# Multiplying the first group's last 256 columns between two pieces of the second group, in a log-softmax backward kernel

## Chip, cores, metric

One core of a Trainium2 chip. The metric is the device time of the whole kernel in microseconds (us), as the median of several executions.

## The reference

```python
# y, dy: (8, 1024, 8192) float32
softmax_x = np.exp(y)
sum_dy = np.sum(dy, axis=-1, keepdims=True)
return (dy - softmax_x * sum_dy).astype(np.float32)
```

Each row needs the sum of its own dy before any of it can be multiplied. 537 MB are read and 268 MB written.

## The kernel before

The 8192 rows are 32 groups of 256 rows, two rows (r = 0, 1) on each of 128 partitions, so a group's dy, y and output are 8.39 MB each. Groups go in pairs: the even one in tile x0, the odd one in x1; one y tile serves both. The product is formed in place in x. All transfers are issued on one queue (SP).

```python
PIECES = [(0, 2048), (2048, 5120), (5120, D)]          # D = 8192, W = 2 * D
def sums(x): ...      # -sum(dy): row 0 on VectorE (reduce), row 1 on ScalarE (two copies that accumulate)
def compute(x, s_t, r):
    for b, e in PIECES:
        cs = slice(r * D + b, r * D + e)
        nc.scalar.activation(y_t[:, cs], y_t[:, cs], EXP)
        nc.vector.scalar_tensor_tensor(out=x[:, cs], in0=y_t[:, cs], scalar=s_t[:, r : r + 1],
                                       in1=x[:, cs], op0=ALU.mult, op1=ALU.add)
for g in range(0, G, 2):
    load_dy(g, x_ts[0])
    load_y(g, 0, W)
    s_t = sums(x_ts[0])
    for r in range(R):
        compute(x_ts[0], s_t, r)
    load_dy(g + 1, x_ts[1])
    s_t = sums(x_ts[1])
    for r in range(R):
        load_y(g + 1, r * D, (r + 1) * D)              # y_t is free once the even group has used it
        compute(x_ts[1], s_t, r)
    for j in range(2):
        nc.sync.dma_start(out=out_v[g // 2, j], in_=x_ts[j][:])
```

In the queue, a pair is: dy even, y even, dy odd, y odd in two halves, store even, store odd.

## Time and profile before

| | before |
|---|---|
| time, median of 4 runs beside the changed kernel | 1866.96 us (1866.79 to 1867.06) |
| span of the profiled run | 1865.3 us |
| busy: DMA queue / VectorE / ScalarE | 99.8% / 46% / 37% |
| one 64 KB row on one DMA engine (single-transfer records) | 2.418 us |
| lost per DMA engine just before the first store's turn | 1.0 us |

The loss in the last row is worked out thus from the trace's records of single transfers: all rows near that point that took over 60 ns more than their undisturbed 2.418 us (64 KB) or 1.213 us (32 KB), their excess summed and divided by the 16 engines. Times from these records count from the span's start, as those of the timelines do.

The prediction shows the main lines. Two more of the same timeline are needed for comparison: the releases of the two next dy loads, each given when a store of the first pair has landed, and then the start of the work on the first of them, when that dy has landed.

```profile
100.95 0.34 SPq L53 DMA_DIRECT2D x<-in_dy_dram  x1
...
120.34 0.33 SPq L53 DMA_DIRECT2D x<-in_dy_dram  x1
...
139.59 8.69 DVE L58 TENSOR_REDUCE s_t<-x 128x1 f32<-128x8192 f32 x1 [46.56 <-DMA x<-in_dy_dram]
```

Columns: start, duration, engine, line, operation. The first store took its turn at about 81 us and had landed by 100.95; the second by 120.34. The dy after them landed at 139.59, 19.25 us after the second store.

### The profile page before, as it was taken

The page shows a single profiled execution, that of the slowest core. Times are in us where ns is not written, and L with a number is a line of the kernel's source. Part 1 is how long each engine was busy: PE and PEld are TensorE (multiplying, and loading weights), DVE is VectorE, ACT ScalarE, POOL GpSimd, SP SyncE. Part 2 cuts the span into 40 slices and gives each one's busy share as a digit, 9 for nine tenths or more (in the row PEclk, how much of TensorE's full clock was granted, in tenths as well). Part 3 has the DMA queues.
Part 4 walks back from the last instruction along what each step waited for, and adds up shares of the span by engine and source line. Part 5 has one row for each costly group of instructions (what it writes and reads, how often), then busy time and mean ns, then how long its engine had stood idle before and what let it go on. Part 6 is the DMA issues. An engine that isn't in the chain of part 4 may idle for free.

```text
span 1865.3 us, 923 instructions
## 1 busy us (share of the span) xinstructions
DVE 859.9 (46%) x256; ACT 698.7 (37%) x321; POOL 0.2 (0%) x4
## 2 busy tenths in 40 slices
DVE  2907429074290732807328063280633806338163
ACT  2606326063260532605326053260523605235152
POOL 0000000000000000000000000000000000000000
DMA  9999999999999999999999999999999999999998
GB/s 427 426 429 427 438 439 427 429 435 441 427 433 443 424 432 444 431 429 429 444 430 430 443 421 438 436 438 429 428 446 429 429 437 428 438 434 440 430 427 387
DMA packets 16135, 805.37 MB, mean 432 GB/s; under 512 B 1792, under 2 KB 1792, under 8 KB 1792
## 3 DMA queue, kind: packets, MB, share of 16 engines
q1 hardware_dynamic: 16128, 805.31, 99.8%
q14 instruction: 7, 0.06, 0.0%
HBM read 536.87 MB, written 268.44 MB: 432 GB/s over the span
## 4 chain that ended last, share of the span: by engine, by line
DMA 64%; DVE 13%; ACT 10%; another core or an unknown queue 10%; issue 1%; SPq 0%; DVEq 0%; ACTq 0%
DMA x<-in_dy_dram 31%; DMA out_dram<-x 30%; DVE x L82 13%; ACT copied L62 6%; ACT y_t L81 4%; DMA y_t<-in_y_dram 3%; SPq L76 0%; DVEq L129 0%; ACTq L129 0%; SPq L53 0%; ACTq L81 0%; ACTq L62 0%
## 5 line engine op out<-in xcount | busy, mean ns | idle before, releaser
L82 DVE SCALAR_TENSOR_TENSOR x<-y_t,s_t,x 128x3072 f32<-128x3072 f32 (+1 forms) x192 | 579.4, 3059 | 255.5 <-ACT y_t L81 255.5
L58 DVE TENSOR_REDUCE s_t<-x 128x1 f32<-128x8192 f32 x32 | 277.8, 8682 | 721.1 <-DMA x<-in_dy_dram 721.1
L81 ACT ACTIVATE y_t<-y_t 128x3072 f32<-128x3072 f32 (+1 forms) x192 | 460.1, 2466 | 268.2 <-DMA y_t<-in_y_dram 241.0
L62 ACT ACTIVATE copied<-x 128x4096 f32<-128x4096 f32 x64 | 229.6, 3587 | 864.7 <-DMA x<-in_dy_dram 863.7
L62 ACT ACTIVATION_READ_ACCUMULATOR copied<-x 128x1 f32 x64 | 11.9, 186 | 0.0
L65 DVE TENSOR_SCALAR s_t<-half_t 128x1 f32<-128x1 f32 x32 | 6.5, 204 | 0.0
L62 ACT ACT_TABLE_LOAD x1 | 1.3, 1283 | 0.7 <-PEq L118 0.7
L118 POOL MEMSET const-bfloat16-1.0<- 128x1 bf16 x1 | 0.1, 101 | 0.0
L118 POOL MEMSET const-uint8-127<- 128x1 uint8 x1 | 0.1, 101 | 0.0
L118 POOL MEMSET const-float32-0.0<- 128x1 f32 x1 | 0.1, 98 | 0.2 <-issue 0.2
L118 POOL MEMSET const-float32-1.0<- 128x1 f32 x1 | 0.1, 98 | 0.0
## 6 DMA issues: line engine op xcount, KB each, us to landing
y_t<-in_y_dram SPq DMA_DIRECT2D x32, 4096.0 KB, 18.4
x<-in_dy_dram SPq DMA_DIRECT2D x32, 48.3
out_dram<-x SPq DMA_DIRECT2D x32, 32.7
y_t<-in_y_dram SPq DMA_DIRECT2D x16, 57.5
```

The lines of the kernel that those rows point to most:

```text
L58: nc.vector.tensor_reduce(out=s_t[:, 0:1], in_=x[:, :D], axis=mybir.AxisListType.X, op=ALU.add, negate=True)
L62: nc.scalar.activation(copied[:], x[:, D + h * H : D + (h + 1) * H], COPY, accum_out=half_t[:, h : h + 1])
L65: nc.vector.tensor_scalar(out=s_t[:, 1:2], in0=half_t[:, 0:1], scalar1=half_t[:, 1:2], scalar2=-1.0, op0=ALU.add, op1=ALU.mult,)
L81: nc.scalar.activation(y_t[:, cs], y_t[:, cs], EXP)
L82: nc.vector.scalar_tensor_tensor(out=x[:, cs], in0=y_t[:, cs], scalar=s_t[:, r : r + 1], in1=x[:, cs], op0=ALU.mult, op1=ALU.add,)
L118: nc = _bacc.Bacc("TRN2", target_bir_lowering=False, num_devices=1)
```

## The change

The intent: in the first pair only, the last 256 columns of the even group get their exp early, into a tile of their own, so that y_t comes free as before. Their multiply is written between the second and third piece of the odd group. The first store needs that multiply, so it should be queued later, behind nothing else new.

```diff
+    LAST = 256
+    SECOND = [(0, 2048), (2048, 3840), (3840, D)]
+    FIRST = [(0, 2048), (2048, 5120), (5120, D - LAST)]
...
-        for r in range(R):
-            compute(x_ts[0], s_t, r)
+        compute(x_ts[0], s_a, 0, PIECES)
+        compute(x_ts[0], s_a, 1, FIRST if first else PIECES)
+        if first:
+            nc.scalar.activation(last_t[:], y_t[:, W - LAST :], EXP)
         load_dy(g + 1, x_ts[1])
         s_t = sums(x_ts[1])
-        for r in range(R):
-            load_y(g + 1, r * D, (r + 1) * D)
-            compute(x_ts[1], s_t, r)
+        load_y(g + 1, 0, D)
+        pieces = SECOND if first else PIECES
+        compute(x_ts[1], s_t, 0, pieces[:2])
+        if first:
+            multiply(x_ts[0], slice(W - LAST, W), last_t[:], s_a, 1)
+        compute(x_ts[1], s_t, 0, pieces[2:])
+        load_y(g + 1, D, W)
+        compute(x_ts[1], s_t, 1, PIECES)
```

More of the change, by code (lines that the diff above doesn't have):

```diff
@@ L49 @@
     y_t = pool.tile([P, W], fp32, name="y_t")
+    last_t = pool.tile([P, LAST], fp32, name="last_t")
     copied = psum.tile([P, H], fp32, name="copied")
@@ L76, in load_y, with multiply, compute @@
         nc.sync.dma_start(out=y_t[:, lo:hi], in_=y_v[g // 2, g % 2][:, lo:hi])
-    def compute(x, s_t, r):
-        for b, e in PIECES:
+    def multiply(x, cs, e_ap, s_t, r):
+        nc.vector.scalar_tensor_tensor(
+            out=x[:, cs],
+            in0=e_ap,
+            scalar=s_t[:, r : r + 1],
+            in1=x[:, cs],
+            op0=ALU.mult,
+            op1=ALU.add,
+        )
+    def compute(x, s_t, r, pieces):
+        for b, e in pieces:
             cs = slice(r * D + b, r * D + e)
             nc.scalar.activation(y_t[:, cs], y_t[:, cs], EXP)
-            nc.vector.scalar_tensor_tensor(
-                out=x[:, cs],
-                in0=y_t[:, cs],
-                scalar=s_t[:, r : r + 1],
-                in1=x[:, cs],
-                op0=ALU.mult,
-                op1=ALU.add,
-            )
+            multiply(x, cs, y_t[:, cs], s_t, r)
     for g in range(0, G, 2):
+        first = g == 0
         load_dy(g, x_ts[0])
         load_y(g, 0, W)
-        s_t = sums(x_ts[0])
-        for r in range(R):
-            compute(x_ts[0], s_t, r)
+        s_a = sums(x_ts[0])
+        compute(x_ts[0], s_a, 0, PIECES)
+        compute(x_ts[0], s_a, 1, FIRST if first else PIECES)
+        if first:
+            nc.scalar.activation(last_t[:], y_t[:, W - LAST :], EXP)
         load_dy(g + 1, x_ts[1])
         s_t = sums(x_ts[1])
-        for r in range(R):
-            load_y(g + 1, r * D, (r + 1) * D)
-            compute(x_ts[1], s_t, r)
+        load_y(g + 1, 0, D)
[6 more added lines that the diff above has]
+        compute(x_ts[1], s_t, 1, PIECES)
         for j in range(2):
```

## The prediction

> **What bounds the kernel now.** I read the page's busy shares first, then the queue table, then the groups by form, and then the timeline of the first pair of groups beside that of the second pair.
>
> ```profile
> DVE 859.9 (46%) x256; ACT 698.7 (37%) x321; POOL 0.2 (0%) x4
> DMA  9999999999999999999999999999999999999998
> q1 hardware_dynamic: 16128, 805.31, 99.8%
> HBM read 536.87 MB, written 268.44 MB: 432 GB/s over the span
> ```
>
> VectorE works 46% of the span and ScalarE 37%; the one hardware queue keeps all 16 DMA engines at work for 99.8% of it. 805.31 MB are 96 transfers of 8.39 MB (32 loads of dy, 32 of y, 32 stores). In the trace's records of single transfers, a 64 KB row takes 2.418 us on its engine, load or store alike, and each engine moves 8 rows per transfer: 96 x 8 x 2.418 = 1857.0 us. The first row starts at 1.7 us, so 1858.8 us of the 1865.3 us span are start and bare movement, whatever order the work has. The other 6.5 us are what order and luck can touch. Those records say where they lie: about 0.6 us of slow first rows at the start; about 1.1 us on every engine at 77 to 81 us; small losses of single engines after that; and the landing and close at the end. Most engines end between 1860.0 and 1861.0 us, but the last row ends at 1864.05. Seven small fetches on another queue (at 279, 320, 879, 882, 1100, 1472 and 1829 us) each cost the one engine that serves them 0.7 to 1.0 us (0.3 us gap, then a row lengthened by 0.4 to 0.7), and the engine that ends last seems to have taken three.
>
> The 1.1 us stall sits exactly where the change works. First pair:
>
> ```profile
> 61.97 8.68 DVE L58 TENSOR_REDUCE s_t<-x 128x1 f32<-128x8192 f32 x1
> 62.08 0.33 SPq L76 DMA_DIRECT2D y_t<-in_y_dram  x1
> 62.45 30.94 SPq L103 DMA_DIRECT2D out_dram<-x  x2
> ...
> 70.93 7.21 ACT L81 ACTIVATE y_t<-y_t 128x2048 f32<-128x2048 f32 x3 [2.26 <-DMA y_t<-in_y_dram]
> 72.87 2.35 DVE L82 SCALAR_TENSOR_TENSOR x<-y_t,s_t,x 128x2048 f32<-128x2048 f32 x1 [2.10 <-ACT y_t L81]
> 75.52 6.75 DVE L82 SCALAR_TENSOR_TENSOR x<-y_t,s_t,x 128x3072 f32<-128x3072 f32 x2 [0.30 <-ACT y_t L81]
> 81.69 7.22 ACT L81 ACTIVATE y_t<-y_t 128x2048 f32<-128x2048 f32 x3 [3.55 <-DMA y_t<-in_y_dram]
> ```
>
> Second pair, the same work:
>
> ```profile
> 178.36 3.59 ACT L62 ACTIVATE copied<-x 128x4096 f32<-128x4096 f32 x1 [5.04 <-DMA x<-in_dy_dram]
> ...
> 179.66 29.83 SPq L103 DMA_DIRECT2D out_dram<-x  x2
> ...
> 197.78 7.22 ACT L81 ACTIVATE y_t<-y_t 128x2048 f32<-128x2048 f32 x3 [2.50 <-DMA y_t<-in_y_dram]
> ```
>
> The columns are start, duration, engine, line and work. The second group's dy lands at 61.22 us in the first pair (ScalarE's first copy starts then) and at 178.36 in the second; the second half of its y lands at 81.69 and 197.78. So 8.39 MB of y took 20.47 us in the first pair and 19.42 in the second: 1.05 us more. In both, the store stood in the queue 1.2 to 1.3 us after that dy had landed, so the store's place in time is not peculiar to the first pair. Only being the first store is. In the single records, the last two 32 KB rows of y on each of the 16 engines are lengthened (1.213 us to about 1.7 each) and the store's own rows then take 2.418 at once.
>
> **What the Trainium skill says.** "DMA: Bandwidth & Descriptors", section "Where 436 GB/s comes from", gives a ceiling of 435.2 GB/s for the 16 ports; the trace's 432 over the whole span (and 65,536 bytes in 2.418 us on 16 engines, 433.6) agrees, so nothing on the compute engines can make the long middle shorter. The same page, "Anatomy of one DMA", says that the DMA engines do not wait on semaphores: the issuing sequencer does, before dispatch. The trace agrees: the queue's sequencer waits for the multiplies (466.1 us in total before stores) and issues later. The section "Queues, rings and completion order" says that each engine consumes its descriptors in ring order; here store rows do follow directly on the last y rows. "VectorE: DVE Perf Modes", section "The TRN2 errata", gives a fixed cost per VectorE and ScalarE instruction; the trace has one:
>
> ```profile
> L82 DVE SCALAR_TENSOR_TENSOR x<-y_t,s_t,x 128x3072 f32<-128x3072 f32 x128 | 431.7, 3414 | 14.5 <-ACT y_t L81 14.5
> L81 ACT ACTIVATE y_t<-y_t 128x3072 f32<-128x3072 f32 x128 | 345.6, 2747 | 0.0
> L82 DVE SCALAR_TENSOR_TENSOR x<-y_t,s_t,x 128x2048 f32<-128x2048 f32 x64 | 150.4, 2350 | 241.0 <-ACT y_t L81 241.0
> L81 ACT ACTIVATE y_t<-y_t 128x2048 f32<-128x2048 f32 x64 | 121.9, 1905 | 268.2 <-DMA y_t<-in_y_dram 241.0 <-DVE s_t L65 27.2
> ```
>
> Between 2048 and 3072 columns the multiply grows by 1064 ns and the exp by 842: 1.039 and 0.822 ns a column, over fixed parts of about 222 and 221 ns.
>
> **The change part by part.** Bytes, number and order of the transfers stay: dy0, y0, dy1, two halves of y1, store 0, store 1, and so on. Pairs 2 to 16 keep every instruction. In the first pair:
>
> 1. One exp of 3072 columns becomes 2816 and 256. ScalarE gains one fixed part, 0.22 us, where it would idle 5 us before the next dy lands. Off the path.
> 2. The last multiply of the first group shrinks by 256 columns, 0.27 us; VectorE's reduce starts at about 61.7 instead of 61.97, and the second half of y is queued 0.05 to 0.3 us sooner, behind 8 us of data in flight. Worth nothing.
> 3. The second group's pieces 3072 + 3072 become 1792 + 4352: the same columns, no time.
> 4. The 256-column multiply moves behind the 1792-column piece. ScalarE has y's first half at 70.93, ends 2048 columns at 72.84 and 1792 (1.69 us) at 74.5. VectorE ends its first piece at 75.22, the second (0.222 + 1792 x 1.039 ns = 2.08 us) at 77.3 and the 256 (0.49 us) at 77.8. The first store is therefore issued at about 77.9 instead of 62.45, 15.4 us later.
> 5. Is that still early enough? At the start, an issue at 0.73 had its first row moving at 1.73, so I take 1.0 us: the rows are ready at about 78.9. The y rows end from 80.63 on now, or from about 79.5 if the stall vanished. The DMA engines don't run dry, by 0.6 to 1.7 us.
> 6. The second group's third piece ends at 77.8 + 4.74 = 82.6 instead of 82.3; its r=1 work starts from the y landing at 81.69 either way and ends near 93.0, while the second store is not needed before 100.95. Hidden.
>
> The certain parts sum to nothing. What remains is whether the 1.05 us stall comes from having the first store queued behind the y load for so long, or from the first store as such.
>
> **The rivals.** *The stall stays or only moves (about 1866.9).* For it: later pairs queue the store equally early and don't stall, so it is the first contact with the output, not the waiting. It began 15 us after the issue and some 3 us before the store's turn, as if the engines look ahead a row or two to the store. If so, they do so at 78.9 as well. *The stall goes (1865.9).* For it: the lengthened rows are those of the load, and the store is behind them only because it was issued early; issued at 77.9 the preparation may find fewer rows to hold up. *The DMA engines run short (1867.5 to 1868.5).* For it: the margin of step 5 rests on one issue at an empty queue, and if preparation for the first store takes 2 us or more with only one or two rows left to hide it, the gap is paid in full by all 16 engines. Against: those margins are positive. *The fetches fall otherwise (1 us either way).* Three more instructions can shift which of the single-engine delays hit the engine that ends last; the three times of before, 1866.79 to 1867.06, show that within one program these are steady.
>
> **Range and chances.** I give 45% to the stall staying, 30% to it vanishing, 25% to a loss of 0.5 to 1.5 us: 0.45 x 1866.9 + 0.30 x 1865.9 + 0.25 x 1867.9 = 1866.85; since a partial gain is also possible I put the time at 1866.6. The range is both ends of the rivals with half a microsecond for fetches: 1865.4 to 1868.2. A change of 2% would be 37 us, two whole transfers of 8.39 MB in which nothing moved; nothing here reaches that, so within 2% is all but certain.
>
> **What would show it.** The issue of the first store near 77.9 us and of the second near 93; the second half of y1 landing at 81.7 (stall stays) or 80.6 (gone); the release of the third group's dy, when the first store has landed, at 100.95, 99.9 or 101.5 and more; and from there a fixed offset to before through all pairs. Busy of the queue should stay at 99.7 to 99.8%. The prediction is wrong if that offset is over 2 us, if later pairs differ in their 116.1 us rhythm, or if the first store is held back past 80.6 us by a wait I overlooked.

## The result and the profile after

The changed kernel took 1867.32 us (1867.05 to 1867.36, 4 runs) beside 1866.96 for before. The ratio is 1.0002, 95% interval 0.9984 to 1.0019: the same. (A ratio is the mean time of one kernel's runs over that of the other's of the same rounds, so not quite the ratio of the medians quoted.) Run again on another chip it gave 1867.31 (1866.99 to 1867.39) beside 1866.78 (1865.93 to 1867.57).

The timeline of the first pair in the changed kernel shows why so little happened:

```profile
53.36 9.03 SPq L82 DMA_DIRECT2D y_t<-in_y_dram  x2
56.01 0.40 ACT L108 ACTIVATE last_t<-y_t 128x256 f32<-128x256 f32 x1
61.41 3.59 ACT L68 ACTIVATE copied<-x 128x4096 f32<-128x4096 f32 x1 [5.00 <-DMA x<-in_dy_dram]
61.90 0.48 DVE L85 SCALAR_TENSOR_TENSOR x<-last_t,s_t,x 128x256 f32<-128x256 f32 x1
62.30 8.68 DVE L64 TENSOR_REDUCE s_t<-x 128x1 f32<-128x8192 f32 x1
62.48 31.15 SPq L120 DMA_DIRECT2D out_dram<-x  x2
...
73.06 4.35 DVE L85 SCALAR_TENSOR_TENSOR x<-y_t,s_t,x 128x2048 f32<-128x2048 f32 x2 [1.96 <-ACT y_t L97]
78.37 4.75 DVE L85 SCALAR_TENSOR_TENSOR x<-y_t,s_t,x 128x4352 f32<-128x4352 f32 x1 [0.96 <-ACT y_t L97]
81.91 7.22 ACT L97 ACTIVATE y_t<-y_t 128x2048 f32<-128x2048 f32 x3 [3.58 <-DMA y_t<-in_y_dram]
...
101.18 0.34 SPq L59 DMA_DIRECT2D x<-in_dy_dram  x1
```

The 256-column multiply (the line that reads `last_t`) ran at 61.90 us, ahead of the odd group's reduce, not after its second piece, which ended at 77.41. Its exp was ready at 56.4, so no data held it back, and the layer that orders instructions while the kernel is built had put it there: in the built program it already stands before the reduce. The first store was issued at 62.48 us, against 62.45 before. A copy of the kernel with that multiply written directly behind its exp, built but not run because nothing could differ, has the same 257 VectorE instructions in the same order. In effect the change splits one exp and one multiply in two, and cuts the odd group's pieces elsewhere.

The stall is there as well. The odd group's dy landed at 61.41 (ScalarE's copy) and its y at 81.91: 20.50 us, 20.47 before. Lost per engine: 1.1 us, between 77.3 and 81.5. Of the 0.23 us by which the release at 101.18 is later, 0.20 had arisen by 42 us: the first exp started at 41.99 instead of 41.79, before any changed instruction ran.

### The profile page after: what moved, and what is told of

The parts are those of the page before. It is cut to its first block, busy times and chain, and to the rows that moved or that the text cites. A ratio compares the mean times of both kernels' runs of the same rounds, so it can differ in the third digit from the quotient of the medians.

```text
span 1865.6 us, 928 instructions
## 1 busy us (share of the span) xinstructions
DVE 860.0 (46%) x257; ACT 698.8 (37%) x322; POOL 0.2 (0%) x4
## 3 DMA queue, kind: packets, MB, share of 16 engines
q1 hardware_dynamic: 16128, 805.31, 99.9%
## 4 chain that ended last, share of the span: by engine, by line
DMA 64%; DVE 13%; ACT 10%; another core or an unknown queue 10%; issue 1%; SPq 0%; DVEq 0%; ACTq 0%
DMA x<-in_dy_dram 31%; DMA out_dram<-x 30%; DVE x L85 13%; ACT copied L68 6%; ACT y_t L97 4%; DMA y_t<-in_y_dram 3%; SPq L82 0%; DVEq L146 0%; ACTq L146 0%; SPq L59 0%; ACTq L97 0%; ACTq L68 0%; SPq L120 0%
## 5 line engine op out<-in xcount | busy, mean ns | idle before, releaser
L85 DVE SCALAR_TENSOR_TENSOR x<-y_t,s_t,x 128x3072 f32<-128x3072 f32 (+2 forms) x192 | 579.2, 3058 | 256.4 <-ACT y_t L97 256.4
L97 ACT ACTIVATE y_t<-y_t 128x3072 f32<-128x3072 f32 (+2 forms) x192 | 459.9, 2465 | 269.1 <-DMA y_t<-in_y_dram 244.2
```

The lines of the kernel that those rows point to most:

```text
L85: nc.vector.scalar_tensor_tensor(out=x[:, cs], in0=e_ap, scalar=s_t[:, r : r + 1], in1=x[:, cs], op0=ALU.mult, op1=ALU.add,)
```

## The experiments

Ten runs were made, eight of edited kernels and two repeats; all gave correct results. The diffs are shortened, some lines joined. In the text, a *turn* is the moment when the DMA engines pass from one transfer in the queue to the next.

### e1_held: the delay made real

```diff
-            multiply(x_ts[0], slice(W - LAST, W), last_t[:], s_a, 1)
+            gate_t = stats.tile([P, R], fp32, name="gate_t")
+            nc.vector.tensor_scalar(out=gate_t[:, 1:2], in0=x_ts[1][:, 3839:3840], scalar1=0.0,
+                                    scalar2=s_a[:, 1:2], op0=ALU.mult, op1=ALU.add)
+            multiply(x_ts[0], slice(W - LAST, W), last_t[:], gate_t, 1)
```

> The changed kernel, but the 256-column multiply takes its scalar from a tiny operation (0.2 us) that reads the last column of the 1792-column piece, so that it cannot be placed before it. All theories: the first store is issued near 78.2 us instead of 62.5. First-contact theory (the stall belongs to the first store, whenever its turn comes): about 1.1 us per DMA engine is still lost, between 79 and 83 us, the third group's dy is released at 101 us as in the changed kernel or up to 1 us later, and the time is 1867 to 1868.5. Queued-early theory (the stall comes from the store standing in the queue behind the y load): no stall, the second half of y1 lands at 80.8 instead of 81.9, release near 100.0, time about 1866.0. Fixed-time theory (the stall has nothing to do with the store): stall at 77.5 to 80 as before, release 101.0, time about 1867.0.

Time 1866.25 us (1866.02 to 1866.31) beside 1866.75 (1865.95 to 1867.43), ratio 0.9996 (0.9982 to 1.001). Timeline of the first pair:

```profile
77.62 0.48 DVE L85 SCALAR_TENSOR_TENSOR x<-last_t,gate_t,x 128x256 f32<-128x256 f32 x1
78.13 14.34 SPq L129 DMA_DIRECT2D out_dram<-x  x2
...
80.76 7.22 ACT L97 ACTIVATE y_t<-y_t 128x2048 f32<-128x2048 f32 x3 [2.50 <-DMA y_t<-in_y_dram]
100.05 0.34 SPq L59 DMA_DIRECT2D x<-in_dy_dram  x1
...
119.79 0.33 SPq L59 DMA_DIRECT2D x<-in_dy_dram  x1
```

And the landing of the next dy, from its later timeline:

```profile
139.68 8.69 DVE L64 TENSOR_REDUCE s_t<-x 128x1 f32<-128x8192 f32 x1 [47.58 <-DMA x<-in_dy_dram]
```

The stall near 78 us is gone: y at 80.76, release at 100.05, 0.90 us sooner than before, as the queued-early theory said. First contact and fixed time fall. But the gain did not last. The next dy landed 19.89 us after the second store (19.25 before), and the records show 0.7 us lost per engine from 116 to 124, where the engines turn from stores to loads, and 0.8 us more at 194 to 197.5, ahead of the second pair's first store. No theory had foreseen those two.

### e2_held_longer: the store comes too late

The gate reads column 8191 of the odd group, and so stands behind the 4352-column piece.

> As e1_held, but the gate reads the last column of the 4352-column piece, so that the first store is issued near 83.3 us, after the last y row has landed. First-contact and queued-early theories: y1's second half lands at about 80.8 with no lengthened rows near 78, because no store stands in the queue; then the DMA engines stand idle from about 80.6 to 84.3, and the third group's dy is released at 103.7 (no stall) to 104.8 (stall paid at the first store itself). Time 1869.5 to 1871. Fixed-time theory: rows at 77.5 to 80 are lengthened by 1.1 us though no store is queued, y1 lands at 81.9.

One run: 1872.57 us, above the range.

```profile
80.68 7.22 ACT L97 ACTIVATE y_t<-y_t 128x2048 f32<-128x2048 f32 x3 [2.49 <-DMA y_t<-in_y_dram]
...
83.76 9.26 SPq L129 DMA_DIRECT2D out_dram<-x  x2
104.56 0.34 SPq L59 DMA_DIRECT2D x<-in_dy_dram  x1
```

No row near 78 us is lengthened, all engines stand idle from 80.2 us, and the first store row starts at 84.61, 0.85 us after the issue (the prediction took 1.0). The later losses of e1_held came too, 0.8 us at 121 and 1.0 at 199; together they are about the size of the miss in the time.

### e3_touch: first contact with the output

```diff
+    nc.vector.memset(touch_t[:], 0.0)               # [128, 128]
...
+            nc.sync.dma_start(out=out_v[0, 0][:, 0:128], in_=touch_t[:])   # between dy and y, first group
```

> The kernel before, with one 512-byte-per-partition store of zeros to the first group's output queued between the first dy and the first y (the real store overwrites it later). First-contact theory: the stall moves to the turn of the small store, about 18 to 22 us, and the y rows near 78 us are not lengthened; time within 0.5 us of before, since the stall is paid once in either place. Queued-early and fixed-time theories: the stall at 77.5 to 80 us stays, and the small store costs 0.1 to 0.5 us.

1867.28 us (1866.5 to 1867.8) beside 1866.75; ratio 1.0002 (0.9989 to 1.0014).

```profile
61.49 3.59 ACT L64 ACTIVATE copied<-x 128x4096 f32<-128x4096 f32 x1 [5.10 <-DMA x<-in_dy_dram]
...
81.73 1.91 ACT L83 ACTIVATE y_t<-y_t 128x2048 f32<-128x2048 f32 x1 [3.31 <-DMA y_t<-in_y_dram]
```

y still took 20.24 us, and 0.8 us per engine was lost before the large store. A small earlier store, and with it the first contact with that output, does not take the stall away.

### e4_shift: everything one transfer later

```diff
+    load_dy(1, x_ts[1])
     for g in range(0, G, 2):
```

> The kernel before with the second group's dy loaded once more at the very start, so that all the rest comes one transfer (19.3 us) later. First-contact and queued-early theories: the stall moves with the first store, to 97 to 100 us, and rows near 78 us have their 2.418 us. Fixed-time theory: rows near 77.5 to 80 us are lengthened (they are then dy rows), those near 97 are not. Time 1886.3 by all.

One run, 1885.70 us, 0.6 below what was expected; why is open. The store is now issued at 81.98:

```profile
81.98 0.43 SPq L104 DMA_DIRECT2D out_dram<-x  x1
...
100.98 4.56 ACT L81 ACTIVATE y_t<-y_t 128x2048 f32<-128x2048 f32 x2 [3.32 <-DMA y_t<-in_y_dram]
```

The lengthened rows moved to 96.7 to 100.6 us (0.8 us per engine). The stall goes with the store.

### e5_swap: with the turn, or so long after the issue?

In e1_held, e4_shift and before, a loss began some 15 us after an issue. This run separates that delay from the turn.

```diff
+            if g == 0 and r == 1:
+                nc.sync.dma_start(out=out_v[0, 0], in_=x_ts[0][:])   # ahead of y's second half
             load_y(g + 1, r * D, (r + 1) * D)
```

> The kernel before, but in the first pair the first store is queued before the second half of y instead of after it, so that its turn comes at about 70.9 us, 9 us after its issue. Turn theory (the DMA engines lose about 1 us when they first go from loads to a large store that already stands in the queue): lengthened rows are those just before the store's turn, between 67 and 71.5 us. Delay theory (the stall comes 15 to 16 us after the issue of the first store, wherever the queue then is): lengthened rows near 77 to 80 us, which are then rows of the store itself. Time 1866 to 1868 by both, since the queue is never empty.

One run, 1867.75 us beside 1867.12.

```profile
62.21 0.35 SPq L101 DMA_DIRECT2D out_dram<-x  x1
...
72.10 7.22 ACT L81 ACTIVATE y_t<-y_t 128x2048 f32<-128x2048 f32 x3 [3.32 <-DMA y_t<-in_y_dram]
```

Lengthened rows: 67.6 to 71.7 us, 1.0 us per engine, in the last rows ahead of the store, 5.4 us after its issue. It is the turn.

### e7_held_less: how early is early?

```diff
-    SECOND = [(0, 2048), (2048, 3840), (3840, D)]
+    SECOND = [(0, 512), (512, 1024), (1024, D)]     # and the gate reads column 1023
```

> As e1_held, but the second group's first half is cut into 512, 512 and 7168 columns and the gate reads the end of the second, so that the first store is issued near 73.9 us: 11.4 us later than in the kernel before and 6 to 7 us before its turn (e1_held: 1.5 to 2.5 us before it). Turn theory: the store is in the queue well before the engines look at it, so the stall of 0.8 to 1.1 us per engine is back near 77 to 81 us, the third group's dy is released at 101.0, and the stalls that e1_held showed near 116 and 194 us are gone or under 0.2 us. Theory that a long stay in the queue causes it: no stall near 78, release at 100.0.

One run, 1866.34 us beside 1867.12.

```profile
73.87 21.35 SPq L129 DMA_DIRECT2D out_dram<-x  x2
...
81.50 7.22 ACT L97 ACTIVATE y_t<-y_t 128x2048 f32<-128x2048 f32 x3 [3.29 <-DMA y_t<-in_y_dram]
100.78 0.34 SPq L59 DMA_DIRECT2D x<-in_dy_dram  x1
```

The stall is back (0.8 us per engine, 77.3 to 81.1), and the losses near 116 and 194 are not seen. A store issued 6.6 us ahead of its turn pays; one issued 1.7 us ahead (e1_held) does not.

### e9_held_two and e8_held_all: does holding save it or put it off?

e1_held's edits, with `first = g < 4` (two pairs) and `first = True` (all sixteen).

> e1_held in the first two pairs only. Turn theory: no stall near 78 and 194 us; the first store that is queued early is then that of the third pair, so about 0.8 us per engine is lost near 308 to 314 us (e1_held: 0.06 there). If the stall near 194 us in e1_held had another cause than the early-queued store, it stays there and nothing is lost near 311.

One run, 1867.83 us. In the third pair, the first whose store is queued early:

```profile
295.21 3.59 ACT L68 ACTIVATE copied<-x 128x4096 f32<-128x4096 f32 x1 [5.09 <-DMA x<-in_dy_dram]
...
315.28 7.22 ACT L97 ACTIVATE y_t<-y_t 128x2048 f32<-128x2048 f32 x3 [3.15 <-DMA y_t<-in_y_dram]
```

y took 20.07 us there, and 0.6 us per engine was lost at 311 to 315. Before the second pair's store next to nothing was lost (0.04 us). The store-to-load turns of the two held pairs cost 0.8 us (116) and 0.5 us (233).

> e1_held in all 16 pairs: every first store of a pair is issued 1.5 to 2.5 us before its turn. Turn theory: no stall before any load-to-store turn (near 78, 194, 311 us under 0.1 us per engine); the one at the first store-to-load turn near 116 to 122 us (0.7 us in e1_held) stays; time 1865.2 to 1866.3. If the margin is too small in some pairs, the DMA engines run short there and each such pair is up to 1 us longer: then slower than before by 1 to 15 us.

1870.30 us (1868.93 to 1871.58, 5 runs) beside 1867.12 (1866.77 to 1867.67): ratio 1.0016 (1.0003 to 1.003). The interval lies wholly above 1, so it is slower, by about 0.16%. By the records, the first stores were issued 0.9 to 1.6 us before their turn. No load-to-store turn stalled and none ran short, but every store-to-load turn lost 0.2 to 0.7 us per engine. Such a turn late in the run, e8_held_all:

```profile
1634.50 0.33 SPq L59 DMA_DIRECT2D x<-in_dy_dram  x1
1654.10 8.69 DVE L64 TENSOR_REDUCE s_t<-x 128x1 f32<-128x8192 f32 x1 [46.89 <-DMA x<-in_dy_dram]
```

and the kernel before:

```profile
1631.56 0.33 SPq L53 DMA_DIRECT2D x<-in_dy_dram  x1
1650.89 8.69 DVE L58 TENSOR_REDUCE s_t<-x 128x1 f32<-128x8192 f32 x1 [46.55 <-DMA x<-in_dy_dram]
```

The dy that follows the stores took 19.60 us against 19.33. The 15 such losses sum to 7.2 us per engine; less the 1.0 us saved at 78 us, a typical engine should end 6.2 us later. The median of the 16 engines' ends is 1866.6 us against 1860.6 in before, 6.0 later. The expected time, 1865.2 to 1866.3, took the first such turn for the only one, and missed.

### Repeats: is anything of this worth having?

The changed kernel and e1_held, unedited, on one chip.

> The changed kernel once more, unedited, to see whether the 0.36 us by which its median lay above before (1867.32 against 1866.96) returns on another chip and another loading. If the change is null, as the compiled order says, its median lies within 0.5 us of before on either side and the two ranges overlap. If the extra instructions do cost something, it lies 0.2 to 0.5 us above again.

1867.31 us (1866.99 to 1867.39) beside 1866.78 (1865.93 to 1867.57), ratio 1.0002 (0.999 to 1.0015). Again 0.4 to 0.5 us above before by the medians, but this time inside before's range (in the first measurement the two ranges only just met, at 1867.05 and 1867.06); whether the extra instructions cost something of that size stays open.

> e1_held once more beside the changed kernel on one chip. If holding the first store is worth its stall, it is 0.5 to 1.0 us below the changed kernel here as well; if the stall is only given back at later turns, as e1_held's trace says (0.7 us at 116 and 0.8 at 194 in place of 1.0 at 78), it lies within 0.5 us of it or above.

1866.38 us (1866.08 to 1867.6), ratio to before 0.9999 (0.9985 to 1.0013). By the medians, 0.9 us below the changed kernel, but not for the reason intended:

| end of the DMA engines' last rows (us), profiled runs | median engine | slowest engine |
|---|---|---|
| before | 1860.6 | 1864.0 |
| changed kernel, two runs | 1860.8, 1860.8 | 1864.3, 1864.3 |
| e1_held, two runs | 1861.3, 1861.4 | 1863.3, 1863.4 |

Holding the store made a typical engine end 0.5 to 0.8 us later. Only the slowest engine ended 0.7 to 1.0 us sooner, and the kernel ends with that one. Why the single-engine delays gather less on it was not tested.

## Why the prediction was right or wrong

The time (1867.32) lies in the range (1865.4 to 1868.2), 0.7 us above the point. That the time fell so near the point was in part luck, because the issue that the prediction reasons about did not move. The working was right in part.

- **Bound: held.** In the changed kernel the queue is busy for 99.9% of the span. Nothing on VectorE or ScalarE showed in the end.
- **Step 1: held.** The separate exp took 0.40 us at 56.0, in ScalarE's idle time.
- **Step 2: the sign was wrong.** The reduce started at 62.30 rather than 61.7, since the 0.48 us multiply ran ahead of it. It cost nothing.
- **Step 4 failed.** "The first store is therefore issued at about 77.9" took the order of the source for the order of execution. It was issued at 62.48. With the order enforced, e1_held issued it at 78.13, which is 77.9 and the 0.22 us of the gate: the sum was sound, its premise was not.
- **Step 5: held where it could be tested.** In e1_held the store rows followed the y rows without a gap; in e2_held_longer the rows moved 0.85 us after the issue, against 1.0 taken.
- **"The stall stays" came true for another reason.** The prediction argued that the stall belongs to the first contact with the output and that engines would look ahead at 78.9 as well. e3_touch takes away the first, e1_held the second. In this kernel the stall stayed because the store had not been delayed.
- **"The stall goes (1865.9)"** was the right rival for a real delay at that turn, but e1_held shows 1866.25 and 1866.38. The rival did not see that the loss comes back at the next turns.

What the runs show together: the first time that the engines turn from loads to a large store that has been in the queue for 6 us or more, each loses 0.6 to 1.1 us (before, the changed kernel, e3, e4, e5, e7; third pair in e9, second pair in e1). After that, load-to-store and store-to-load turns cost under 0.3 us on average over the engines. As long as it has not happened, each store-to-load turn costs 0.2 to 0.8 us (e1, e2, e9, and all of e8). So in these runs about 1 us is paid once, at the first store that is queued early, and holding stores costs more than it saves on a typical engine. That the first such turn is what settles the later ones is not shown: in every run the held pairs came first, so a rival fits as well, in which holding a pair's first store itself causes the loss at that pair's own store-to-load turn. A run that holds a later pair alone would tell them apart; none was made. The mechanism is open: no run looked inside the engines, and how far apart the 16 engines start their rows before the turn does not explain it (within 0.43 us in before's first pair and 0.85 us in e1_held's second, both with a loss, but 0.62 us in before's second pair without one).

## What to carry to other kernels

The place of an instruction in the source is no schedule: if a step must wait, give it a data dependence on what it should wait for, and look in the timeline for the moment when it ran before judging the idea. In a kernel whose DMA queue is over 99% busy, follow a saved stall to the end of the trace, because the same loss can come back at later turns, and the end is set by the slowest of the 16 engines, not by the average.

## What the Trainium skill lacked or had wrong

- "DMA: Bandwidth & Descriptors" has nothing on the cost of a turn between loads and stores on one busy queue. Here the first load-to-store turn with the store queued 6 us ahead or more cost 0.6 to 1.1 us per engine on average; with the store issued 0.9 to 1.6 us ahead in every pair, each store-to-load turn cost 0.2 to 0.7 us.
- "Runtime: NRT & Kernel Launch", section "Instruction fetch mechanics", calls the cost of refilling an engine's instruction memory mostly hidden. In this DMA-bound kernel each of the seven instruction packets in the profile of before took 0.7 to 1.0 us from the one DMA engine that served it. The slowest DMA engine ended 3.5 us after the median one (1864.0 against 1860.6); how many of the seven fell on it was not settled.
